# A decoder block on one core: GpSimd's element-wise work on VectorE, attention's loads a step sooner, the last block's end in two groups of positions

## The chip, the cores and the metric

The kernel runs on one core of one Trainium2 chip. The metric is the device time of one execution in microseconds; several runs are taken and their median is compared. The engines are called as the profile calls them: PE (TensorE), DVE (VectorE), ACT (ScalarE), POOL (GpSimd) and SP (SyncE, which issues the DMAs).

## The reference

One block of a hybrid decoder over 2048 positions of width 1024, in float32. A projection of the normalised input feeds gated linear attention (4 heads, in chunks) and a short gated convolution side by side; both go through one output projection and are added to the input; a SwiGLU feed-forward layer of width 2816 follows, and a last RMSNorm.

```python
h = rmsnorm(x, norm1_g[l])
proj = h @ w_in[l]
p_q, p_k, p_v, p_g, p_a, c_b, c_c, c_h = jnp.split(proj, splits, axis=-1)
...
gate_logits = (p_a @ w_gate_up[l] + b_gate[l]).astype(jnp.float32)
log_a = (jax.nn.log_sigmoid(gate_logits) / GATE_NORMALIZER).reshape(bsz, seq, GLA_HEADS, GLA_DK)
o = gla_chunked(q, k, v, log_a)
o = rmsnorm(o, gla_norm_g[l]).astype(x.dtype)
o = o * jax.nn.silu(p_g.reshape(bsz, seq, GLA_HEADS, GLA_DV))
...
o_conv = c_b * causal_depthwise_conv(u, conv_w[l])
```

After that come `x + concat(o_gla, o_conv) @ w_out`, the second norm, `silu(h @ w_gate) * (h @ w_up)` times `w_down` added to it, and the last norm.

## The kernel before

The 2048 positions are four blocks of 512; two blocks make a half. The stages run in the order opening, in_proj of half 0, in_proj of half 1 with the attention of half 0 beside it, the attention of half 1 beside out_proj(0), out_proj(1), then ffn_up and ffn_down of half 0 and of half 1, and `last_unit`, the last two columns of features of half 1 with the final norm.

All large products are float32 made of two parts in the faster format: every operand is split into a high part (ACT, line 193) and the rest (DVE, line 194), and each step is three matmuls (lines 460 to 462; 1220, 1221 and 1223 in out_proj) of 128x512. `unit` computes a 2 by 2 arrangement of blocks with seven products in place of eight, so sums and differences of operands are made ahead: `combine` (its `subtract`, line 359) for the normalised input, lines 1332 to 1336 in `ffn_up` for the feed-forward's hidden values, line 435 for the weights. Results leave the eight PSUM banks through ACT (line 500) or DVE (line 489).

The order of instructions on each engine is made once, when the program is built: a scheduler with an estimate of times merges the streams, and each engine then runs its list strictly in turn. SP issues every load (line 148) and store (line 151) in one such list. Side work, such as attention and norms, stands in generators in `background`; `tick()` takes one step of them between products. The step counts therefore decide where in PE's list a chunk stands.

Attention, `gla_half`, takes 8 chunks of 128 positions per half. A step makes the scores of a chunk, the next one finishes the chunk before (`gla_finish`: transposes `ot`, line 1178, gate, split, store to `sgla`), loads the next chunk (`gla_load`: 14 loads, two exponentials on ACT, lines 1105 and 1106, and two multiplications on DVE) and makes this chunk's outputs. `gate` and `forget_gate` (lines 1011 to 1024) make the decays that these loads read. out_proj(1) reads attention back from `sgla` as `op`.

The sums of squares for a norm: ACT squares a column (line 1201) and POOL adds it to `ssx` (line 1202); a matmul with ones (`rs` or `tot`) adds over features, and the factor is spread by transposes `rb_ps`. `last_unit` computes two columns for block 2 (j = 0), then for block 3 (j = 1), each of 18 matmuls of 128x512, sums squares, and scales all eight columns of each block before storing them (line 1480).

## Time and profile before

| | us |
|---|---|
| median of 3 runs | 2055.72 (2054.32 to 2055.76) |
| the profiled execution | 2050.15, span 2048.4, clock 0.996 |
| busy: PE, DVE, ACT, POOL | 2021.6, 1549.0, 971.7, 335.4 |
| opening and in_proj(0), to about | 250 |
| in_proj(1) with attention of half 0, to about | 475 |
| attention of half 1 beside out_proj(0), out_proj(1) from about | 667 |
| feed-forward, half 0 | 755 to 1380 |
| feed-forward, half 1 | 1380 to 2010 |
| `last_unit`'s last matmul of a column | 2033.2 |

The span is the time between the first and the last instruction of the profiled execution, so it is a little under that execution's own time. The rows of the profile name line, engine, operation and tiles; "idle before" with an arrow tells what ended the engine's wait.

### The profile page before, as it was taken

To read this page: it belongs to the slowest core of one execution; us is meant where nothing else is said; L and a number is where in the kernel's file an instruction comes from. 1 tells how busy PE (TensorE), PEld (TensorE's weight loads), DVE (VectorE), ACT (ScalarE), POOL (GpSimd) and SP (SyncE) were. 2 spreads that over 40 slices of the span, in tenths; PEclk is the share of its full clock that TensorE was granted. 3 is DMA by queue.
4 is the path that set the end of the run, shared out by engine and by line. 5 is a ranking of instruction groups with operands and counts; after the bars stand their busy time and mean duration, and the time that the engine had idled before them with its cause. 6 is when DMAs were issued, how large, how long until landed. Compare 5 with 4: busy or idle time off the path is not lost.

```text
span 2048.4 us, 26987 instructions
## 1 busy us (share of the span) xinstructions
PE 2021.6 (99%) x9271; PEld 1662.2 (81%) x9271; DVE 1549.0 (76%) x2533; ACT 971.7 (47%) x1930; POOL 335.4 (16%) x218
## 2 busy tenths in 40 slices
PE   9999999999999999999999999999999999999997
PEld 8788878887888888888788888877888888888886
DVE  7888967558744797778777688877777768778884
ACT  6664556755533344444444452334534443453344
POOL 0000000000002451222222112200311321211213
PEclk9999999999999999999999999999999999999998
DMA  7356886425586873546445576576444434586663
GB/s 262 123 201 215 295 301 188 132 85 160 180 307 233 324 270 134 194 150 216 176 145 193 212 285 250 188 277 273 155 169 170 167 136 170 185 328 221 236 231 114
DMA packets 189738, 422.54 MB, mean 206 GB/s; under 512 B 19904, under 2 KB 65184, under 8 KB 180128
## 3 DMA queue, kind: packets, MB, share of 16 engines
q1 hardware_dynamic: 189600, 420.81, 58.5%
q8 instruction: 73, 1.20, 0.2%
q14 instruction: 65, 0.53, 0.1%
HBM read 276.02 MB, written 144.70 MB: 205 GB/s over the span
## 4 chain that ended last, share of the span: by engine, by line
PE 87%; DVE 4%; DMA 4%; ACT 2%; issue 1%; SPq 1%; POOL 0%; DVEq 0%; ACTq 0%; POOLq 0%
PE mm L460 25%; PE mm L462 25%; PE mm L461 25%; PE mm L1220 2%; PE mm L1221 2%; PE mm L1223 2%; DMA raw<-in_wffn_dram 1%; DVE wq L194 1%; DVE h L894 1%; PE a_ps L976 1%; PE mm L756 1%; PE mm L758 1%; PE mm L757 1%; DMA raw<-in_win_dram 1%; PE o_ps L1144 1%
## 5 line engine op out<-in xcount | busy, mean ns | idle before, releaser
L460 PE MATMUL mm<-op,wq 128*128 128x512 f32 x2467 | 961.5, 392 | 10.9 <-ACT c L500 5.0
L461 PE MATMUL mm<-op,wq 128*128 128x512 f32 x2467 | 959.7, 390 | 0.2 <-DVE op L194 0.2
L462 PE MATMUL mm<-op,wq 128*128 128x512 f32 x2467 | 948.7, 390 | 0.9 <-DVE wq L194 0.6
L193 ACT ACTIVATE wq<-raw 128x512 fp32r<-128x512 f32 (+2 forms) x612 | 355.7, 587 | 582.5 <-PE mm L462 461.3
L194 DVE TENSOR_TENSOR wq<-raw,wq 128x512 fp32r<-128x512 f32 (+2 forms) x612 | 446.8, 736 | 165.1 <-ACT wq L193 163.5
L460 PEld LDWEIGHTS mm<-op,wq 128*128 128x128 f32 x2467 | 463.5, 188 | 115.3 <-ACT c L500 6.8
L462 PEld LDWEIGHTS mm<-op,wq 128*128 128x128 f32 x2467 | 463.5, 188 | 99.6 <-DVE wq L194 2.7
L461 PEld LDWEIGHTS mm<-op,wq 128*128 128x128 f32 x2467 | 463.6, 188 | 96.4 <-DVE op L194 1.7
L1202 POOL TENSOR_TENSOR ssx<-ssx,q 128x512 f32<-128x512 f32 x52 | 75.7, 1473 | 866.4 <-ACT q L1201 866.2
L489 DVE TENSOR_TENSOR c<-mm,c 128x512 f32<-128x512 f32 x196 | 134.6, 687 | 52.3 <-PE mm L462 44.9
L489 DVE TENSOR_TENSOR y<-mm,y 128x512 f32<-128x512 f32 x185 | 126.3, 686 | 47.8 <-PE mm L462 47.5
L435 DVE TENSOR_TENSOR raw<-raw 128x512 f32<-128x512 f32 (+2 forms) x192 | 151.9, 794 | 2.9
L1336 POOL TENSOR_TENSOR t<-c,c 128x512 f32<-128x512 f32 x44 | 74.4, 1690 | 434.8 <-DVE c L1332 406.9
L500 ACT ACTIVATE c<-mm 128x512 f32<-128x512 f32 x198 | 115.6, 587 | 17.5 <-PE mm L462 13.9
L435 DVE TENSOR_TENSOR s<-raw 128x512 f32<-128x512 f32 (+2 forms) x96 | 62.0, 645 | 52.0 <-DMA raw<-in_wffn_dram 36.5
L1220 PE MATMUL mm<-op,wq 128*128 128x512 f32 x256 | 101.2, 396 | 0.0
L1221 PE MATMUL mm<-op,wq 128*128 128x512 f32 x256 | 99.7, 390 | 0.0
L193 ACT ACTIVATE wq<-s 128x512 fp32r<-128x512 f32 (+2 forms) x96 | 56.3, 586 | 90.9 <-PE mm L462 88.2
L1418 POOL TENSOR_TENSOR y<-x,y 128x512 f32<-128x512 f32 x32 | 57.7, 1803 | 230.4 <-DVE y L489 181.3
L1223 PE MATMUL mm<-op,wq 128*128 128x512 f32 x256 | 80.0, 390 | 0.0
L435 DVE TENSOR_TENSOR raw<-s,raw 128x512 f32<-128x512 f32 (+2 forms) x96 | 69.8, 727 | 2.0
L552 ACT ACTIVATE c<-c 128x512 f32<-128x512 f32 x78 | 49.2, 631 | 34.7 <-DVE c L489 32.7
(229 smaller groups left out, 1788.5 us busy)
## 6 DMA issues: line engine op xcount, KB each, us to landing
raw<-in_wffn_dram SPq DMA_DIRECT2D x44, 1024.0 KB, 6.1
sa_B<-so SPq DMA_DIRECT2D x47, 512.0 KB, 4.3
op<-sa_B SPq DMA_DIRECT2D x47, 512.0 KB, 6.9
raw<-in_win_dram SPq DMA_DIRECT2D x22, 1024.0 KB, 5.5
sa_T<-so SPq DMA_DIRECT2D x44, 512.0 KB, 3.8
op<-sa_T SPq DMA_DIRECT2D x44, 512.0 KB, 6.4
raw<-in_wdown_dram SPq DMA_DIRECT2D x24, 768.0 KB, 5.8
sx<-y SPq DMA_DIRECT2D x48, 256.0 KB, 4.4
```

Source lines behind the costliest of these rows:

```text
L193: last_hi[:] = [act.activation(hi, src, AF.Copy)]
L194: last_lo[:] = [dve.tensor_tensor(lo, src, hi.bitcast(F32), ALU.subtract)]
L435: dve.tensor_tensor(*args)
L460: pe.matmul(o[:], wh, xh, start=first and k == 0, stop=False, skip_group_check=True)
L461: pe.matmul(o[:], wh, xl, start=False, stop=False, skip_group_check=True)
L462: return pe.matmul(o[:], wl, xh, start=False, stop=k == n - 1, skip_group_check=True)
L489: last_plus[:] = [dve.tensor_tensor(t[:], o[:], t[:], ALU.add)]
L500: last_out[:] = [act.activation(t[:], o[:], AF.Copy)]
L1202: pool.tensor_tensor(ssq[:], ssq[:], q[:], ALU.add)
L1220: pe.matmul(o[e, j][:], wh, m[:, 0, :], start=k == 0, stop=False)
L1221: pe.matmul(o[e, j][:], wh, m[:, 1, :], start=False, stop=False)
L1223: pe.matmul(o[e, j][:], wl, ops[k][j][:, 0, :], start=False, stop=k == KD - 1)
```

## The change

Six edits: (1) `subtract` in `combine`, (2) the sums of squares, (3) the four differences of `ffn_up` and (4) the last add of `ffn_down` go from POOL to DVE. (5) `gla_load` is cut in two: `gla_fetch` issues the loads, a step sooner, right behind the scores of the chunk before and ahead of `gla_finish`; `gla_scaled` has the exponentials and multiplications and stays where they were; one more `yield` stands at the start. (6) `last_unit` is written anew with an order of its own on each engine: block 2 (`j0`) as a whole, then the first 256 positions of block 3 (`p0`) and the last 256 (`p1`) one after the other. POOL keeps two sums and eight scales there, and stores are issued from SP and ACT.

```diff
 
         def subtract(y, a, b):
             with behind(last_plus if with_marks else []):
-                (dve if with_marks else pool).tensor_tensor(y, a, b, ALU.subtract)
+                dve.tensor_tensor(y, a, b, ALU.subtract)
 
         fetch()
         fetch()
@@ -1075,19 +1075,22 @@
         chunks = [(b, t) for b in (2 * half, 2 * half + 1) for t in range(PT)]
         with tc.issue_after(last_silu[0].ins):
             tables = act.preload_act_table_set("natural_log_exp_and_others")
+        fetched = gla_fetch(*chunks[0])
+        yield
         with tc.issue_after(tables.ins):
-            nxt = gla_load(*chunks[0])
+            cur = gla_scaled(*fetched)
         yield
         o = None
         for n, (b, t) in enumerate(chunks):
-            cur = nxt
             s = gla_scores(b, t, *cur)
             yield
+            if n + 1 < len(chunks):
+                fetched = gla_fetch(*chunks[n + 1])
             if o is not None:
                 yield from gla_finish(*chunks[n - 1], *o)
+            o = gla_outputs(b, t, *s)
             if n + 1 < len(chunks):
-                nxt = gla_load(*chunks[n + 1])
-            o = gla_outputs(b, t, *s)
+                cur = gla_scaled(*fetched)
             yield
         yield from gla_finish(b, t, *o)
         done.add((b, t))
@@ -1096,12 +1099,15 @@
     decays = {}
     done = set()
 
-    def gla_load(b, t):
+    def gla_fetch(b, t):
         s = slice(t * P, (t + 1) * P)
         kq, e, vt, g = [bt(n, (P, 4, P)) for n in ("kq", "ee", "vt", "gt")]
         for dst, src in ((kq, s_kq[b]), (e[:, 2:4, :], s_d[b]), (vt, s_v[b]), (g, s_g[b])):
             for i, r in enumerate(src):
                 load(dst[:, i, :], r[:, s])
+        return kq, e, vt, g
+
+    def gla_scaled(kq, e, vt, g):
         act.activation(e[:, 0:2, :], e[:, 2:4, :], AF.Exp, scale=-1.0 / 16.0)
         act.activation(e[:, 2:4, :], e[:, 2:4, :], AF.Exp, scale=1.0 / 16.0)
         dve.tensor_tensor(kq[:, 0:2, :], kq[:, 0:2, :], e[:, 0:2, :], ALU.mult)
@@ -1199,7 +1205,7 @@
         else:
             q = tt("q")
             act.activation(q[:], y, AF.Square)
-            pool.tensor_tensor(ssq[:], ssq[:], q[:], ALU.add)
+            dve.tensor_tensor(ssq[:], ssq[:], q[:], ALU.add)
 
     def build_mix(half):
         def pair(b, k):
@@ -1333,7 +1339,7 @@
             b11, b12, b21, b22 = [sg[r, j] for r in range(2) for j in range(2)]
             t1, t2, t3, t4 = [bt(n) for n in ("t1", "t2", "t3", "t4")]
             for y, p, q in ((t1, b12, b11), (t2, b22, t1), (t3, b22, b12), (t4, b21, t2)):
-                pool.tensor_tensor(y[:], p[:], q[:], ALU.subtract)
+                dve.tensor_tensor(y[:], p[:], q[:], ALU.subtract)
             values = [("B11", b11), ("B21", b21), ("B22", b22)]
             if half == 1 and m >= LAST_GROUP:
                 values.append(("B12", b12))
@@ -1415,7 +1421,7 @@
                     elif last:
                         store(s_x1[2 * half + j][d0 + r][:], yy)
                 for yy, x1 in xs:
-                    pool.tensor_tensor(yy, x1[:], yy, ALU.add)
+                    dve.tensor_tensor(yy, x1[:], yy, ALU.add)
         if half == 0:
             ahead[:] = [finish_later(half)]
 
@@ -1444,86 +1450,169 @@
...
+        HB = PB // 2
+        parts = {"j0": (0, 0, PB), "p0": (1, 0, HB), "p1": (1, HB, HB)}
+        order = {}
+        def then(eng, issue):
+            with behind([order[eng]] if eng in order else []):
+                order[eng] = issue()
+            return order[eng]
...
+        def spread(part, copied=True):
+            rb = rbs[part] = bank("rb_ps")
+            j, _, n = parts[part]
+            with behind([order[pe]]):
+                for t in range(n // P):
+                    order[pe] = pe.transpose(
+                        rb[:, t * P : (t + 1) * P], reps[part][:, t, :], ident[:]
+                    )
+            if copied:
+                copy_of(part)
+        def copy_of(part):
+            j, _, n = parts[part]
+            copies[part] = ssq[j][:, sl(part)]
+            then(act, lambda: act.activation(copies[part], rbs[part][:, 0:n], AF.Copy))
+        def scale(part, d, eng, queue):
+            j, _, n = parts[part]
+            by = rbs[part][:, 0:n] if eng is dve else copies[part]
+            yy = y[d, j][:, sl(part)]
+            then(eng, lambda: eng.tensor_tensor(yy, yy, by, ALU.mult))
+            with behind([order[act]] if queue is nc.scalar else []):
+                queue.dma_start(out[2 + j, :, d, sl(part)], yy)
+        def columns_of(part, r):
+            j, _, n = parts[part]
+            o = bank()
+            with behind([order[pe]] if pe in order else []):
+                for i in range(2):
+                    p = columns[j][i]
+                    for k in range(len(b12)):
+                        cs = slice(k * P, (k + 1) * P)
+                        wq = w[2 * r + i]
+                        for wi, xi in ((0, 0), (0, 1), (1, 0)):
+                            order[pe] = pe.matmul(
+                                o[:, 0:n], wq[:, wi, cs], p[k][:, xi, sl(part)],
+                                start=i == 0 and k == 0 and wi + xi == 0,
+                                stop=i == 1 and k == len(b12) - 1 and wi == 1,
+                                skip_group_check=True,
+                            )
+            return o
...
+        taken("j0", 0, columns_of("j0", 0))
+        summed("j0", 0, pool)
+        gained_in("j0", 0)
+        taken("j0", 1, columns_of("j0", 1))
+        summed("j0", 1, dve)
+        gained_in("j0", 1)
+        taken("p0", 0, columns_of("p0", 0))
+        summed("p0", 0, pool)
+        add_up("j0", ssq[0])
+        factors("j0")
+        gained_in("p0", 0)
+        taken("p0", 1, columns_of("p0", 1))
+        spread("j0")
+        summed("p0", 1, dve)
+        gained_in("p0", 1)
+        scale("j0", 0, dve, sp)
+        for d in (2, 4, 5, 6):
+            scale("j0", d, pool, sp)
+        taken("p1", 0, columns_of("p1", 0))
+        add_up("p0", ssq[1])
+        factors("p0", lambda: scale("j0", 1, dve, sp))
+        gained_in("p1", 0)
+        summed("p1", 0, dve)
+        o = columns_of("p1", 1)
+        spread("p0", copied=False)
+        add_up("p1", ssq[1], last=False)
+        taken("p1", 1, o)
+        add_up("p1", q[1, 1], first=False)
+        for d in (3, 7):
+            scale("j0", d, dve, sp)
+        factors("p1", *[partial(scale, "p0", d, dve, sp) for d in (0, 1)])
+        copy_of("p0")
+        gained_in("p1", 1)
+        for d in (2, 5, 6, 7):
+            scale("p0", d, pool, ac)
+        scale("p0", 3, dve, sp)
+        spread("p1", copied=False)
+        scale("p0", 4, dve, sp)
         for d in range(KD):
+            scale("p1", d, dve, ac if d % 2 else sp)
```

The functions left out keep their work: `add_up` sums over features, `factors` makes the reciprocal root and its copy `rep` for one part, `taken` adds a column and squares it, `summed` adds the squares up.

Line numbers move by 6 in the attention and out_proj code (1105 becomes 1111, 1179 becomes 1185, 1245 becomes 1251, 1202 becomes 1208). POOL's list falls from 205 rows to 16.

On ACT, in the list around the second gate: `L1105` and `L1106` (then `L1111` and `L1112`) are the exponentials of a chunk, `L500` the eviction of a PSUM bank, `L193` splits. Before:

```order
L193 ACTIVATE wq<-raw 128x512 [waits DVE_49]
L193 ACTIVATE wq<-raw 128x512 [waits PE_49]
L193 ACTIVATE wq<-raw 128x512 [waits DMAHW7_49,PE_49]
L1023 ACTIVATE el<-g_4745 128x4 [waits DVE_49]
L1105 ACTIVATE ee<-ee 128x256 [waits DMAHW5_49,DMAHW4_49]
L1106 ACTIVATE ee<-ee 128x256 [waits Activation_49]
L500 ACTIVATE c_4872<-mm 128x512 [waits DVE_49]
L1021 ACTIVATE em<-g_4842 128x4 [waits DVE_49]
```

and now:

```order
L500 ACTIVATE c_4854<-mm 128x512 [waits DVE_49,PE_49]
L1023 ACTIVATE el<-g_4724 128x4 [waits DVE_49]
L1014 ACTIVATE g_4824<-g_4824,ones 128x512 [waits Activation_49]
L193 ACTIVATE wq<-raw 128x512 [waits DVE_49]
L193 ACTIVATE wq<-raw 128x512
L1014 ACTIVATE g_4871<-g_4871,ones 128x512 [waits Activation_49]
L193 ACTIVATE wq<-raw 128x512 [waits DMAHW7_49,PE_49]
L1111 ACTIVATE ee<-ee 128x256 [waits DMAHW5_49,DMAHW4_49]
L193 ACTIVATE wq<-s_4971 128x512 [waits PE_49]
L1112 ACTIVATE ee<-ee 128x256 [waits Activation_49]
```

The eviction that stood right behind a pair of exponentials, and so behind their load, now stands ahead of the next pair; splits of weights stand behind and between them.

On DVE, where attention ends and out_proj(0) runs out: `osb<-ot` takes the last chunk's transposes, `osb<-osb,gt` makes the part that is stored, `y<-y,mm` are out_proj's evictions. Before:

```order
L1171 TENSOR_TENSOR osb<-o_ps,hsq 128x512
L1245 TENSOR_TENSOR y<-y,mm 128x512 x4
L1179 SCALAR_TENSOR_TENSOR osb<-ot,sml,gt 128x512
L194 TENSOR_TENSOR wq<-raw,wq 128x512
L194 TENSOR_TENSOR osb<-osb,gt 128x512
L194 TENSOR_TENSOR wq<-raw,wq 128x512 x3
L1245 TENSOR_TENSOR y<-y,mm 128x512 x4
L194 TENSOR_TENSOR wq<-raw,wq 128x512 x3
L256 TENSOR_SCALAR rb_6780<-tot 128x512
```

and now:

```order
L1185 SCALAR_TENSOR_TENSOR osb<-ot,sml,gt 128x512
L194 TENSOR_TENSOR osb<-osb,gt 128x512
L194 TENSOR_TENSOR wq<-raw,wq 128x512
L1251 TENSOR_TENSOR y<-y,mm 128x512 x3
L1208 TENSOR_TENSOR ssx_5989<-ssx_5989,q 128x512
L1251 TENSOR_TENSOR y<-y,mm 128x512
L1208 TENSOR_TENSOR ssx_5990<-ssx_5990,q 128x512
L194 TENSOR_TENSOR wq<-raw,wq 128x512
L1208 TENSOR_TENSOR ssx_5989<-ssx_5989,q 128x512
L1208 TENSOR_TENSOR ssx_5990<-ssx_5990,q 128x512
L194 TENSOR_TENSOR wq<-raw,wq 128x512
L256 TENSOR_SCALAR rb_6780<-tot 128x512
```

Before, two columns of out_proj's evictions (x4 each) stand around or behind the last chunk's rows and further ones follow; now one column follows and the sums of squares, which POOL had, stand between. On PE the last chunk's four transposes stand 96 large matmuls ahead of out_proj(1)'s first one before, and 37 now.

On PE, the end of the program: `rs` sums squares over features, `rb_ps` are the transposes that spread the factors, the other rows are a column's matmuls. Before:

```order
L461 MATMUL mm<-op,wq 128x512
L462 MATMUL mm<-op,wq 128x512
L460 MATMUL mm<-op,wq 128x512
L461 MATMUL mm<-op,wq 128x512
L462 MATMUL mm<-op,wq 128x512
L1454 MATMUL rs<-ones,q 128x1 [waits Activation_49]
L1454 MATMUL rs<-ones,q 128x1 x3
L1474 MATMUL rb_ps<-ident,rep 128x128 [waits DVE_49]
L1474 MATMUL rb_ps<-ident,rep 128x128 x3
```

and now:

```order
L1541 MATMUL mm<-op,wq 128x256 x18
L1481 MATMUL rs<-ones,ssx_17441 128x1 [waits DVE_49]
L1481 MATMUL rs<-ones,ssx_17441 128x1
L1541 MATMUL mm<-op,wq 128x256 x18
L1511 MATMUL rb_ps<-ident,rep 128x128 [waits DVE_49]
L1511 MATMUL rb_ps<-ident,rep 128x128
L1481 MATMUL rs<-ones,ssx_17441 128x1 [waits DVE_49]
L1481 MATMUL rs<-ones,ssx_17441 128x1
L1481 MATMUL rs<-ones,q 128x1 [waits Activation_49]
L1481 MATMUL rs<-ones,q 128x1
L1511 MATMUL rb_ps<-ident,rep 128x128 [waits DVE_49,PE_49]
L1511 MATMUL rb_ps<-ident,rep 128x128
```

The last column is 18 matmuls of 256 positions, and what follows the last matmul is two rows for each thing where there were four; the other 256 positions' transposes stand there too.

119 lines of the change are left out of this document (53 added, 66 removed).

## The prediction

> **What bounds the kernel now.** I read the page's first part, then the chain of waits, the waits by engine, the busy time by stage, and the timelines of the three places that the change reorders.
>
> ```profile
> PE 2021.6 (99%) x9271; PEld 1662.2 (81%) x9271; DVE 1549.0 (76%) x2533; ACT 971.7 (47%) x1930; POOL 335.4 (16%) x218
> PE 87%; DVE 4%; DMA 4%; ACT 2%; issue 1%; SPq 1%; POOL 0%; DVEq 0%; ACTq 0%; POOLq 0%
> ```
>
> TensorE is busy 99% of the span and makes 87% of the chain that ended last; POOL has no share in the chain. So work that leaves POOL gains nothing by itself. Time can only come from PE's idle time, from what lies behind PE's last matmul, or from the number and speed of matmuls.
>
> ```profile
> PE mm L460 <- ACT c L500: 5.0, 3, 3.0
> PE mm L460 <- ACT wq L193: 1.2, 3, 0.5
> PE rs L226 <- POOL ssx L1202: 0.3, 1, 0.3
> ...
> 645.00:667.00 22.00, 22.00 (x100) 18.21 (x98) 8.06 (x11) 4.84 (x10) 5.77 (x4) 1.00 1.01 360
> 667.00:755.00 88.00, 88.00 (x386) 72.17 (x385) 71.32 (x78) 35.21 (x60) 47.29 (x30) 1.00 0.90 317
> 755.00:1380.00 625.00, 623.11 (x2750) 513.25 (x2749) 493.49 (x751) 267.61 (x489) 131.37 (x80) 1.00 0.56 200
> ```
>
> The waits (total us, times, longest) are few; the largest is one stall of 3.0 us behind an eviction on ACT (L500). Of all POOL work PE waited 0.3 us. In the stage rows the columns after the window's length are PE, weight loads, DVE, ACT and POOL busy, then the clock, the DMA share and GB/s; 88.00/386 gives 0.228 us per matmul of 128x512.
>
> **1. The gate, at 473 us.**
>
> ```profile
> 472.31 0.79 SPq L148 DMA_DIRECT2D ee<-sd  x2
> 474.79 0.42 ACT L1105 ACTIVATE ee<-ee 128x256 f32<-128x256 f32 x1 [1.02 <-DMA ee<-sd]
> 475.56 0.58 ACT L500 ACTIVATE c<-mm 128x512 f32<-128x512 f32 x1
> 476.19 0.53 PE L460 MATMUL mm<-op,wq 128*128 128x512 f32 x1 [3.01 <-ACT c L500]
> 476.20:479.60 3.40, 3.40 (x9) 2.68 (x10) 3.40 (x8) 0.21 (x1) 0.00 (x0) 0.55 0.43 104
> ```
>
> ACT stands at the exponentials of a chunk whose load was issued only at 472.31; behind them in its queue is the eviction for which PE waits. That costs PE 3.01 us. Then the clock falls: in the next 3.40 us, at a granted clock of 0.55, 9 matmuls run where 3.40/0.228 = 15 would, so 6 x 0.228 = 1.4 us more. Together 4.4 us. The change fetches the chunk a step sooner, and in its ACT order that eviction stands ahead of the exponentials. A chunk's 14 loads at 0.79/2 = 0.4 us are 5.5 us of SP's queue; they now stand ahead of the previous chunk's two stores, which wait that much and which nobody reads before out_proj. Against the gain: weight splits (L193 wq) now stand behind the exponentials, on which PE also waits, and the whole attention moves a step later, so all its meetings are dealt anew. As the price of those I take 1.0, near the 1.2 us that all waits on such splits cost before. Term: -3.4 (bounds -4.4, and 0 if another wait fully takes its place).
>
> The Trainium skill, "TensorE: Matmul & The Clock Gate", section "What's actually happening", says that the array falls to half clock after an idle window of about 3.4 us. The trace agrees about so (a wait of 3.01 us sufficed); by that rule waits of under 3 us cost only themselves.
>
> **2. The end of attention, at 645 us.** The extra step of the attention generator pushes its last chunk behind: before, the last transposes `ot` stand 96 matmuls ahead of out_proj(1)'s first; in the change's PE order 37. So the slack falls from 96 x 0.228 = 21.9 to 37 x 0.228 = 8.4 us, plus three matmuls on the other block before the first that reads the new data: 9.1.
>
> ```profile
> 644.64 0.60 PE L1178 MATMUL ot<-ident,osb 128*128 128x128 f32 x4
> 645.87 0.74 DVE L1179 SCALAR_TENSOR_TENSOR osb<-ot,sml,gt 128x512 f32<-128x512 f32 x1
> 646.67 0.62 ACT L193 ACTIVATE gt<-osb 128x512 fp32r<-128x512 f32 x1
> 647.84 1.77 DVE L194 TENSOR_TENSOR osb<-osb,gt 128x512 fp32r<-128x512 f32 x1
> 649.64 0.51 SPq L151 DMA_DIRECT2D sgla<-osb  x1
> 653.08 3.66 SPq L148 DMA_DIRECT2D op<-sgla  x7
> DMA to landing us min/median/max: 3.4/6.0/6.9
> DMA to landing us min/median/max: 6.0/10.5/11.3
> ```
>
> What must pass in it: eviction, split on ACT and DVE, store, load. Before, from the end of `ot` at about 645.1 to the earliest landing of a load at 653.08 + 6.0 = 659.1 it took 14.0 us, hidden within 21.9. (The last two rows are landing times of the `sgla` transfers in 649 to 654 and of the `op` loads from 653 on.) At its best: 0.3 to start, 0.74 + 0.62 + 0.69 (the split without POOL beside it, as other 512-wide DVE rows below), 0.3 between them, 3.4 for the store and 3.4 for the load: 9.4. So PE waits 0.3 to 4.9 us, and at the long end the half clock adds 1.4: 0.3 to 6.3. I take +2.0, nearer the low end, since POOL no longer stretches the split (1.77 to 0.69) and DVE's rows just ahead of it are short. Later loads follow at the rate at which PE uses them, so the wait comes once.
>
> **3. POOL's work on DVE.** 52 sums of squares, 88 subtracts of ffn_up, 32 adds of ffn_down and 32 subtracts of `combine`: 204 operations.
>
> ```profile
> L1202 POOL TENSOR_TENSOR ssx<-ssx,q 128x512 f32<-128x512 f32 x52 | 75.7, 1473 | 866.4 <-ACT q L1201 866.2
> L1336 POOL TENSOR_TENSOR t<-c,c 128x512 f32<-128x512 f32 x44 | 74.4, 1690 | 434.8 <-DVE c L1332 406.9 <-DMA sa_B<-so 27.9
> L1418 POOL TENSOR_TENSOR y<-x,y 128x512 f32<-128x512 f32 x32 | 57.7, 1803 | 230.4 <-DVE y L489 181.3 <-DMA x<-sx 48.5 <-ACT wq L193 0.6
> ...
> L489 DVE TENSOR_TENSOR y<-mm,y 128x512 f32<-128x512 f32 x185 | 126.3, 686 | 47.8 <-PE mm L462 47.5
> L194 DVE TENSOR_TENSOR wq<-raw,wq 128x512 fp32r<-128x512 f32 x422 | 336.0, 801 | 155.0 <-ACT wq L193 153.8
> L435 DVE TENSOR_TENSOR raw<-raw 128x512 f32<-128x512 f32 x130 | 116.3, 897 | 1.9
> L194 DVE TENSOR_TENSOR op<-t,op 128x512 fp32r<-128x512 f32 x8 | 9.4, 1172 | 2.4 <-ACT op L193 2.2
> ```
>
> On DVE such an operation takes 0.686 us (the row of L489) where POOL takes 1.5 to 1.8: 204 x 0.686 = 139.9 us more on DVE. But DVE operations with two SBUF inputs are longer than 686 ns on the mean, and only while POOL runs beside them: 422 x 0.115 + 130 x 0.211 + 8 x 0.486 = 48.5 + 27.4 + 3.9 = 79.8 us in these three rows alone, which should vanish with POOL's work. DVE then goes from 1549 to at most 1549 + 139.9 - 79.8 = 1609 us, 79% of the span. The tightest stage is 667 to 755: 71.3 + 30 x 0.686 = 91.9 us, more than its 88, if nothing got shorter; less the 3.9 (all eight are there) and POOL's share of the rest there, 47.3/335.4 x 75.9 = 10.7, it is 77.3. It fits. In 755 to 1380: 493.5 + 80 x 0.686 = 548 of 625 without any relief. So I cost this part at 0: PE's matmuls cover it. What it costs if the cover is gone is the second rival. Gone is only the wait on POOL's `ssx`: -0.3. Bounds: -4 (the small waits of the FFN also vanish) to +4 (the 91.9 - 88 of the tight stage).
>
> **4. The end.**
>
> ```profile
> 2032.74 12.21 SPq L151 DMA_DIRECT2D out_dram<-y  x15
> ...
> 2033.40 0.25 PE mm L462
> 2033.75 0.69 DVE L1508 TENSOR_TENSOR y<-mm,y 128x512 f32<-128x512 f32 x1 [0.49 <-PE mm L462]
> 2034.47 0.63 ACT L1511 ACTIVATE q<-y 128x512 f32<-128x512 f32 x1 [3.13 <-DVE y L1508]
> 2035.16 1.05 PE L1454 MATMUL rs<-ones,q 128*128 128x1 f32 x8 [1.52 <-ACT q L1511]
> 2037.46 0.43 DVE L1467 COPY rep<-py 128x512 f32<-128x512 f32 x1
> 2037.94 1.12 PE L1474 MATMUL rb_ps<-ident,rep 128*128 128x128 f32 x4 [1.73 <-DVE rep L1467]
> 2039.79 3.68 DVE L1480 TENSOR_TENSOR y<-y,rb_ps 128x512 f32<-128x512 f32 x6 [1.90 <-ACT ssx L1475]
> out_dram<-y SPq DMA_DIRECT2D x16, 256.0 KB, 2.5
> L460 PEld LDWEIGHTS mm<-op,wq 128*128 128x128 f32 x2467 | 463.5, 188 | 115.3 <-ACT c L500 6.8
> ```
>
> Now the last column ends at 2033.65 and the run 2048.4: 14.75 us of add, square, sum, factors, transposes, 8 scales and 16 stores. In the change only 256 positions go through that at the end. Halving what depends on the width: add 0.1 + 0.35; square 0.05 + 0.42 (an exponential of 256 in part 1's fence took that); four sums 0.53 + 0.05; factors from the end of `rs`, 2036.22, to the transposes, 2037.94: 1.72, less half the copy's 0.43 is 1.50; two transposes 0.56; eight scales between half of 3.68/6 and 0.42: 8 x 0.36 = 2.9; last store's issue 0.45, landing 2.5; and 1.0 to the run's end, as before (2032.74 + 12.21 + 2.5 = 2047.45, against 2048.4). With 0.5 between steps: 10.9 us, so -3.85. The other half's and the first block's stores, 3 MB, must be out before: at the 360 GB/s of 645 to 667 that is 8.7 us, and by the order they start two narrow columns, some 4.3 us, ahead of the last column's end and are out at +4.4, when the last scales start. POOL's four scales of 256 run beside DVE's and may stretch them, bound +1.
>
> PE's stream itself: fewer `rs` ahead of the last column (6 rows in the order instead of 12, each two matmuls in the trace at 1.05/8 = 0.13): 6 x 2 x 0.13 = 1.6 at half clock; at the full clock they are shorter, I take -1.3. 36 matmuls of 512 become 72 of 256, each weight loaded twice. At half the time each nothing changes; if the weight load of 0.188 us sets the pace it is 72 x 0.188 - 36 x 0.228 = +5.3. Against that: the eight `rs` matmuls, each with a 128x128 weight load of its own, come 0.13 apart at half clock, so 0.188 is a load's length and not its pace. I take 0.12 each, +0.5. Term: -1.3 + 0.5 - 3.85 = -4.6 (bounds -6 to +1.7).
>
> The Trainium skill, "TensorE: Matmul & The Clock Gate", sections "LDWEIGHTS (loading the stationary operand)" and "Back-to-back issue gap", gives 107 ns for a load of 128 columns and 262 cycles, 109 ns, for 256 columns of matmul. By it the 72 would take an estimated 7.9 us, no more than the 36; no run here shows a 256-wide one.
>
> **Sum.** -3.4 + 2.0 - 0.3 + 0 - 4.6 = -6.3 us. The profiled execution took 2050.15 us around its span of 2048.4 and lies 5.6 under the median of the runs. Taken off the profiled one it gives 2043.9; off the median of 2055.7, which is what is measured, 2049.4.
>
> **The rivals.**
>
> *Attention's end takes back what its start gives.* The wait in part 2 at its long end, 6.3, and a split that takes the place of the gate's stall (0 for -3.4): +6.3 - 0.3 - 4.6 = +1.4, 2057. For it: 9.1 us of slack against 14.0 as measured. Against: the stretched split and 1 us of DVE queue in those 14.0.
>
> *DVE's queue blocks: slower.* POOL could sit idle for its inputs at no cost; DVE takes its work in order. Of POOL's idle time 27.9 us ended with a store of `so` and 48.5 with a load of `x` (rows of part 3). Where such a wait now stands in DVE's queue, weight splits and evictions stand behind it. The 48.5 us are 1.5 per add, and a column of 24 matmuls lasts 5.5, so a late eviction is hidden as long as other banks are free; it decides from the point where a wait exceeds about one column. If a fifth of the 76.4 us comes through, +15: 2055.7 - 6.3 + 15 = 2064. Against: PE's waits on DVE are all under 2 us now, and the stages have 12% to spare.
>
> *Narrow matmuls paced by weight loads*: +4.8 on the sum, 2054.2.
>
> *The FFN's small waits go too*, as DVE's operations are shorter: -4 more, 2045.4. For it: PE loses a few us in waits on `c` and `wq` there; against: they are redealt, not removed.
>
> **How the numbers follow.** Forecast 0.50, attention's end 0.18, DVE's queue 0.14, weight loads 0.08, FFN 0.10. What this measurement tells from no change is 0.2%, 4.1 us. Faster by more: most of the forecast and all of the FFN case, 0.43 + 0.10, and little of the others: 0.55. Same: 0.07 of the forecast, 0.10 of attention's end, 0.07 of the weight loads: 0.24. Slower: 0.21. The forecast's own range is 2046 to 2053 (the gate's 0 to -4.4 and the end's bounds). For 8 in 10 it is widened to the FFN case below and past attention's end above, with part of DVE's queue: 2043.5 to 2060.
>
> **What would show it.** Gate: no PE idle over 1 us behind L500 near 473 and no window under full clock there. Attention's end: a PE wait on a load of `op<-sgla` at out_proj(1) of about 2 us. DVE: L194's mean for 128x512 near 690 ns, DVE's busy time under 1610, POOL with some ten operations. End: last column to end near 11 us, and 18 matmuls of 256 in 2.0 to 2.2 us. I am wrong if PE's waits on DVE rows, or on weights split late, grow by 6 us or more, or if the 256-wide matmuls take over 0.15 us each.

## The result, and the profile after

| | before | after |
|---|---|---|
| median, us | 2054.38 (2050.22 to 2055.76, 6 runs) | 2043.03 (2041.94 to 2045.20, 6 runs) |
| ratio | | 0.9951, 95% interval 0.9941 to 0.9961 |
| profiled execution, us | 2050.15, span 2048.4 | 2043.05, span 2041.3 |

The change is faster by 10.1 us by the ratio (8.0 to 12.1); 6.3 were forecast. The ratio is not the quotient of the two medians, which lie 11.4 us apart; differences below go by the ratio unless medians are named. The median lies 0.5 us under the low end of the forecast's range, and the kernel before ran 1.3 us under the 2055.7 from which the forecast was taken off. The page of the changed kernel, its busy times and its chain:

```profile
PE 2016.8 (99%) x9295; PEld 1661.9 (81%) x9295; DVE 1534.8 (75%) x2752; ACT 976.4 (48%) x1936; POOL 11.0 (1%) x17
PE 92%; DMA 3%; DVE 3%; ACT 1%; issue 0%; SPq 0%; DVEq 0%; ACTq 0%
```

POOL has gone from 335.4 us to 11.0, and DVE, with 219 operations more (POOL's 204 and some of the new end), is busy for 14 us less. The waits of PE (total, times, longest) and two stages of the same profile (window, its length, then PE, weight loads, DVE, ACT, POOL, clock, DMA share, GB/s):

```profile
PE mm L460 <- ACT c L500: 4.2, 5, 1.7
PE rb_ps L1511 <- DVE rep L1503: 2.7, 2, 2.4
PE mm L460 <- ACT op L193: 2.1, 1, 2.1
PE mm L462 <- DVE wq L194: 1.2, 1, 1.2
...
PE rs L1481 <- DVE ssx L1566: 1.0, 1, 1.0
...
PE mm L1226 <- DMA op<-sgla: 0.4, 1, 0.4
```

```profile
667.00:755.00 88.00, 88.00 (x385) 72.01 (x385) 68.01 (x110) 33.71 (x56) 0.00 (x0) 1.00 0.97 353
755.00:1380.00 625.00, 624.19 (x2762) 515.74 (x2761) 486.45 (x835) 271.05 (x493) 0.00 (x0) 1.00 0.56 203
```

The stall of 3.0 us behind L500 is gone, and the longest such wait is 1.7; the forecast wait on `op<-sgla` is there with 0.4 us. Two lines belong to the end, both waits on DVE: the one on `rep` was there before with 1.7 and has grown to 2.7, the one on `ssx` is new. The row of `op` from L193, at 271 us, has the same 2.1 in the kernel before.

Where the 7.1 us between the two profiled spans went, from the times at which PE reaches the same places (read from the timelines; each place is the first matmul of its kind there):

| stretch | before, us | after, us | difference |
|---|---|---|---|
| start to the gate matmul of half 0 | 89.41 | 89.97 | +0.56 |
| to the last matmul of out_proj(1) | 666.06 | 664.89 | -1.17 |
| to the first spread of the second norm | 29.81 | 28.35 | -1.46 |
| to the second spread | 31.76 | 31.76 | 0 |
| the rest of half 0's feed-forward and the start of half 1's, to the final norm's first spread | 690.94 | 688.59 | -2.35 |
| to the last column's last matmul | 525.26 | 524.19 | -1.07 |
| last matmul's start to the end of the span | 15.19 | 13.58 | -1.61 |

So the gain is spread over four places (the last two rows are both the end), and 3 us more of the ratio lie in runs that these two profiles don't show. The experiments take these apart.

### The profile page after: what moved, and what is told of

The parts are those of the page before. It is cut to its first block, busy times and chain, and to the rows that moved or that the text cites. A ratio compares the mean times of both kernels' runs of the same rounds, so it can differ in the third digit from the quotient of the medians.

```text
span 2041.3 us, 26875 instructions
## 1 busy us (share of the span) xinstructions
PE 2016.8 (99%) x9295; PEld 1661.9 (81%) x9295; DVE 1534.8 (75%) x2752; ACT 976.4 (48%) x1936; POOL 11.0 (1%) x17
## 4 chain that ended last, share of the span: by engine, by line
PE 92%; DMA 3%; DVE 3%; ACT 1%; issue 0%; SPq 0%; DVEq 0%; ACTq 0%
PE mm L460 25%; PE mm L462 25%; PE mm L461 25%; PE mm L1226 3%; PE mm L1227 3%; PE mm L1229 3%; PE mm L756 1%; PE a_ps L976 1%; PE mm L757 1%; PE mm L758 1%; PE o_ps L1148 1%; PE o_ps L1150 1%; PE mm L1541 1%; DVE wq L194 0%; PE sc L1124 0%
## 5 line engine op out<-in xcount | busy, mean ns | idle before, releaser
L193 ACT ACTIVATE wq<-raw 128x512 fp32r<-128x512 f32 (+2 forms) x612 | 357.4, 588 | 602.1 <-PE mm L462 486.7
L460 PEld LDWEIGHTS mm<-op,wq 128*128 128x128 f32 x2443 | 458.5, 188 | 109.6 <-ACT c L500 6.4
L462 PEld LDWEIGHTS mm<-op,wq 128*128 128x128 f32 x2443 | 458.5, 188 | 98.6 <-DVE wq L194 2.7
L461 PEld LDWEIGHTS mm<-op,wq 128*128 128x128 f32 x2443 | 458.7, 188 | 95.2 <-DVE op L194 1.5
L194 DVE TENSOR_TENSOR wq<-raw,wq 128x512 fp32r<-128x512 f32 (+2 forms) x612 | 386.0, 636 | 179.6 <-ACT wq L193 178.2
L500 ACT ACTIVATE c<-mm 128x512 f32<-128x512 f32 x198 | 115.3, 589 | 20.7 <-PE mm L462 16.7
L435 DVE TENSOR_TENSOR raw<-raw 128x512 f32<-128x512 f32 (+2 forms) x192 | 120.3, 632 | 2.2
L193 ACT ACTIVATE wq<-s 128x512 fp32r<-128x512 f32 (+2 forms) x96 | 56.4, 587 | 103.7 <-PE mm L462 98.0
L435 DVE TENSOR_TENSOR s<-raw 128x512 f32<-128x512 f32 (+2 forms) x96 | 60.8, 633 | 35.6 <-DMA raw<-in_wffn_dram 20.0
L194 DVE TENSOR_TENSOR op<-op 128x512 fp32r<-128x512 f32 x94 | 62.0, 684 | 3.6 <-ACT op L193 3.5
L194 DVE TENSOR_TENSOR wq<-s,wq 128x512 fp32r<-128x512 f32 (+2 forms) x96 | 60.8, 633 | 3.3 <-ACT wq L193 2.5
L435 DVE TENSOR_TENSOR raw<-s,raw 128x512 f32<-128x512 f32 (+2 forms) x96 | 60.8, 634 | 1.4
L193 ACT ACTIVATE op<-op 128x512 fp32r<-128x512 f32 x94 | 54.6, 620 | 7.2 <-DMA op<-sa_T 3.7
L1226 PEld LDWEIGHTS mm<-op,wq 128*128 128x128 f32 x256 | 48.1, 188 | 11.3 <-issue 1.6
```

The lines of the kernel that those rows point to most:

```text
L193: last_hi[:] = [act.activation(hi, src, AF.Copy)]
L194: last_lo[:] = [dve.tensor_tensor(lo, src, hi.bitcast(F32), ALU.subtract)]
L435: dve.tensor_tensor(*args)
L460: pe.matmul(o[:], wh, xh, start=first and k == 0, stop=False, skip_group_check=True)
L461: pe.matmul(o[:], wh, xl, start=False, stop=False, skip_group_check=True)
L462: return pe.matmul(o[:], wl, xh, start=False, stop=k == n - 1, skip_group_check=True)
```

## The experiments

The edits are numbered as in the change: (1) `combine`, (2) sums of squares, (3) and (4) the feed-forward's differences and adds, (5) attention's loads, (6) the end. Every kernel was timed beside the kernel before on the same chip.

| run | what | median, us | ratio to before |
|---|---|---|---|
| e1 | before, again | 2053.24 | 0.9999 (0.9991 to 1.0008) |
| e2 | (1) to (4) | 2048.41 | 0.9981 (0.9969 to 0.9993) |
| e3 | (5) | 2055.89 | 1.0014 (1.0005 to 1.0023) |
| e4 | (6) | 2051.55 | 0.9988 (0.9979 to 0.9997) |
| e5 | (1) to (4), (6) | 2046.38 | 0.9965 (0.9953 to 0.9977) |
| e6 | (1) to (5) | 2045.88 | 0.9964 (0.9952 to 0.9976) |
| e7 | (1), (2), (5) | 2046.45 | 0.9965 (0.9953 to 0.9977) |
| e8 | (1), (5) | 2047.91 | 0.9975 (0.9965 to 0.9984) |
| the change | (1) to (6) | 2043.03 | 0.9951 (0.9941 to 0.9961) |
| e9 | change, one add of the end on PE | 2042.67 | 0.9945 (0.9932 to 0.9958) |
| e10 | e9, copies of the end on ACT | 2044.18 | 0.9949 (0.9936 to 0.9962) |
| e11 | change, end without POOL | 2044.56 | 0.9954 (0.9940 to 0.9969) |
| e12 | (1), (2), (5), (6) | 2046.27 | 0.9966 (0.9954 to 0.9978) |

### The kernel before, again, and what its runs differ by

No edit.

> The kernel before, unchanged, for its spread (2050.2 to 2055.8 so far) and a second profile. Theory A: the runs at 2054 to 2056 carry one or two stalls that the profiled one of 2050.15 did not have, and this profile shows where (a PE wait of some us, or a second piece of half clock). Theory B: they are slower evenly, by clock or by opening, with no single place. Ratio to before 1.000.

The second profile has a span of 2051.5 us, 3.1 more than the first. Two short windows of it, with the same columns as above:

```profile
274.12:277.53 3.41, 3.22 (x8) 2.54 (x9) 3.41 (x7) 3.05 (x6) 0.00 (x0) 0.50 1.04 377
478.92:482.33 3.41, 3.19 (x8) 2.51 (x9) 3.41 (x9) 0.38 (x2) 0.00 (x0) 0.50 0.42 119
```

The second piece of half clock is the one of the prediction, behind the stall at the gate. The first isn't in the earlier profile: it follows a wait of 2.45 us for `op` at 271, where half 1's projection begins. In the earlier profile that wait is 2.10 us (the row of `op` from L193 shown above, which the prediction's rows leave out). It stands in every profile taken here (1.7 to 2.7 us); with the half clock after it in all but the first one of before and the one of the change. The piece costs about 3.41 x 0.5 = 1.7 us; the rest of the 3.1 is 0.8 in the first 90 us and 0.8 in a longer wait at 310. Theory A holds in the main, as far as one more profile shows it: the first profile of before is one of its better executions, so beside it the change gains 7.1 us and beside the runs 10.1.

### POOL's work on DVE alone

Edits (1) to (4), such as

```diff
-                pool.tensor_tensor(y[:], p[:], q[:], ALU.subtract)
+                dve.tensor_tensor(y[:], p[:], q[:], ALU.subtract)
```

> Only POOL's 204 operations on DVE, attention's loads and the end as before. If the sum of the prediction holds (0, bounds -4 to +4): 2050 to 2055 in the median, DVE busy under 1610 us, L194 of 128x512 near 690 ns. Theory B, that this part carries the gain since operations that POOL no longer stretches release stalls of the feed-forward: 2045 to 2049. Rival of DVE's blocked queue: over 2058.

This is theory B's range. By the ratio it is -3.9 us (-6.4 to -1.4). DVE's splits and sums in this profile, and the tightest stage:

```profile
L194 DVE TENSOR_TENSOR wq<-raw,wq 128x512 fp32r<-128x512 f32 x422 | 289.7, 688 | 159.3 <-ACT wq L193 157.4
...
667.00:755.00 88.00, 88.00 (x386) 72.14 (x386) 70.00 (x113) 36.54 (x61) 0.00 (x0) 1.00 0.94 343
```

801 ns have become 688, and the tight stage holds 35 operations more at 1.3 us less of busy time (71.32 before). No blocked queue shows. On PE's path the stretch to the second norm's spread is 28.37 us (29.79 in the second profile of before), and the feed-forward of half 0 688.69 (691.04): 3.8 us together, which is the whole gain by the ratio.

### Attention's loads alone

Edit (5).

```diff
+            if n + 1 < len(chunks):
+                fetched = gla_fetch(*chunks[n + 1])
             if o is not None:
                 yield from gla_finish(*chunks[n - 1], *o)
```

> Only attention's loads a step sooner, POOL and the end as before. By the prediction -3.4 + 2.0 and by the trace after about -2.6: 2051 to 2053, with no stall at the gate, and with POOL stretching the last split (1.8 us) a wait on op<-sgla of 1 to 3 us. If the loads alone carry nothing (another stall takes the place): 2054 to 2056.

The median lies in the second range, and as it says another stall takes the place; but the loads don't carry nothing, they cost 2.9 us (1.0 to 4.7). The gate's stall is gone as foreseen, and a worse one stands at 762. The wait on `op<-sgla` is 0.40 us where 1 to 3 were expected. The timeline of this run:

```profile
750.07 1.74 POOL L359 TENSOR_TENSOR t<-h,t 128x512 f32<-128x512 f32 x1
751.83 0.33 SPq L151 DMA_DIRECT2D sfT<-t  x1
...
755.74 2.62 SPq L148 DMA_DIRECT2D h<-sfB  x4
758.00 3.91 ACT L193 ACTIVATE op<-h 128x512 fp32r<-128x512 f32 x6 [2.96 <-DMA h<-sfB]
763.05 0.61 ACT L193 ACTIVATE wq<-raw 128x512 fp32r<-128x512 f32 x1
763.71 0.50 PE L460 MATMUL mm<-op,wq 128*128 128x512 f32 x1 [2.03 <-ACT wq L193]
766.39 1.75 DVE L194 TENSOR_TENSOR wq<-raw,wq 128x512 fp32r<-128x512 f32 x1
768.20 0.80 PE L462 MATMUL mm<-op,wq 128*128 128x512 f32 x1 [3.75 <-DVE wq L194]
```

Read it from the bottom. PE waits for a weight split; the split stands on ACT behind six splits of `op<-h`; these wait for loads, and the loads stand in SP's queue behind the store of POOL's last difference, made at 750 to 752. The waits of 2.03 and 3.75 us and 6.8 us of half clock behind them make the stretch to the second norm's spread 36.3 us where it was 29.8.

### The end alone

Edit (6).

```diff
+        parts = {"j0": (0, 0, PB), "p0": (1, 0, HB), "p1": (1, HB, HB)}
...
+                                o[:, 0:n], wq[:, wi, cs], p[k][:, xi, sl(part)],
```

> Only the end in two groups of positions, the rest as before. By the trace after it is worth 14.75 - 13.3 us behind the last column and 1.2 us on PE ahead of it, 2.7 us: 2051 to 2052. If the end is worth what was predicted (4.6): 2049 to 2050.

By the ratio -2.5 us (-4.3 to -0.6); last matmul to end 13.64 us, as in the change. It is the smaller of the two sizes.

### The change without the loads, and without the end

The whole change without edit (5), with one yield and one call as before:

```diff
-        fetched = gla_fetch(*chunks[0])
-        yield
         with tc.issue_after(tables.ins):
-            cur = gla_scaled(*fetched)
+            nxt = gla_load(*chunks[0])
```

> The change without its edit on attention's loads (POOL's work on DVE and the new end). Theory A, the parts add up: -5.4 of DVE alone and -2.3 of the end alone from 2053.8 give 2046.1, with the gate's stall of about 3 us still there. Theory B, the loads carry nothing even with DVE: as the whole change, 2043.

2046.38: the parts add up, 0.9981 x 0.9988 = 0.9969 beside 0.9965. So beside DVE's edits and the new end the loads are worth 0.9951/0.9965, 2.9 us, and alone they cost as much. The two intervals overlap by 0.0008; e6 below beside e2, which also differ in the loads alone, gives 3.5 us the same way.

The whole change without edit (6), `last_unit` as before:

```diff
-            scale("p1", d, dve, ac if d % 2 else sp)
+            scale(1, d, None if d in (2, 5) else rb1)
```

> The change without its new end. Theory A: the whole change's 2043.0 plus 2.3 to 2.7 for the end, 2045.3 to 2045.7, last column to end 14.7 us. If the end is worth more once DVE is free of POOL (4.6 as predicted): 2047.6.

2045.88: 2.9 us above the change, 2.7 by the ratios, with intervals that overlap. The end alone gave 2.5, and e5 beside e2 gives 3.3. So the end is worth about the same with DVE free of POOL as without, 2.5 to 3.3, and 4.6 appears in none of the three.

### What makes the loads slow alone

Edits (5), (1) and (2): the feed-forward stays on POOL.

```diff
-                (dve if with_marks else pool).tensor_tensor(y, a, b, ALU.subtract)
+                dve.tensor_tensor(y, a, b, ALU.subtract)
...
-            pool.tensor_tensor(ssq[:], ssq[:], q[:], ALU.add)
+            dve.tensor_tensor(ssq[:], ssq[:], q[:], ALU.add)
```

> Attention's loads a step sooner, and of POOL's work only what belongs to norms (the differences of combine and the sums of squares) on DVE; the feed-forward's differences and adds stay on POOL, the end as before. Theory A, that the loads alone were slow since splits of weights stood on ACT behind six splits that waited for loads of what POOL had made late (waits of 2.0 and 3.8 us at 761 to 768 and half clock after them): no such wait, 2046 to 2049. Theory B, that the later attention itself makes these waits: they stay, 2053 to 2056.

No wait of PE is left at 750 to 770, and the median is 2046.45.

Edits (5) and (1) alone: the first two lines of that diff.

> Attention's loads a step sooner and of POOL's work only the differences of combine on DVE. If it is these differences, on POOL, that came late: no wait over 1 us at 761 to 768, 2047 to 2050. If it is the sums of squares beside them that stretch DVE's splits there (1.75 in place of 0.69 us): a wait of 2 to 4 us stays, 2051 to 2055.

2047.91. The same place in this run, DVE making the last difference:

```profile
747.25 0.68 DVE L359 TENSOR_TENSOR t<-h,t 128x512 f32<-128x512 f32 x1
747.96 0.32 SPq L151 DMA_DIRECT2D sfT<-t  x1
...
748.85 3.93 SPq L148 DMA_DIRECT2D h<-sfB  x4
751.78 2.64 ACT L193 ACTIVATE op<-h 128x512 fp32r<-128x512 f32 x4 [1.09 <-DMA h<-sfB]
...
762.32 0.50 PE L462 MATMUL mm<-op,wq 128*128 128x512 f32 x1 [1.01 <-DVE wq L194]
```

The last difference is stored 3.9 us sooner, at 747.96 where it was 751.83, and ACT gets past its six splits some 5 us sooner; PE's 5.8 us of waits shrink to 1.0. So it is the differences of `combine`, 32 operations, that turn the loads from a loss into a gain. That they do it by coming sooner is read from these rows: the order of ACT's list changes with the edit as well. With the sums of squares on DVE as well (e7) the last 1.0 goes there too; the two medians lie 1.5 us apart, within the intervals.

### The end, taken apart

The timeline of the end of the changed kernel:

```profile
2024.34 5.07 POOL L1526 TENSOR_TENSOR y<-y,ssx 128x512 f32<-128x512 f32 x4 [3.16 <-ACT ssx L1520]
2025.65 2.38 PE L1541 MATMUL mm<-op,wq 128*128 128x256 f32 x18
2027.35 0.94 DVE L1503 COPY rep<-py 128x256 f32<-128x256 f32 x1
2028.21 1.48 DVE L1566 TENSOR_TENSOR ssx<-ssx,q 128x256 f32<-128x256 f32 x1
2029.61 0.41 DVE L1555 TENSOR_TENSOR y<-mm,y 128x256 f32<-128x256 f32 x1
2029.74 0.61 PE L1481 MATMUL rs<-ones,ssx 128*128 128x1 f32 x4 [0.96 <-DVE ssx L1566]
2032.48 2.83 POOL L1526 TENSOR_TENSOR y<-y,ssx 128x256 f32<-128x256 f32 x4 [3.07 <-ACT ssx L1520]
2032.49 0.86 DVE L1503 COPY rep<-py 128x256 f32<-128x256 f32 x1
2033.50 0.66 PE L1511 MATMUL rb_ps<-ident,rep 128*128 128x128 f32 x2 [2.37 <-DVE rep L1503]
```

The last column ends at 2028.0. Its eviction (L1555) could start then and starts at 2029.61, behind a copy and an add that run while POOL does its four scales. In e9 PE adds up these squares instead:

```diff
-        summed("p1", 0, dve)
...
         add_up("p1", ssq[1], last=False)
+        add_up("p1", q[1, 0], first=False, last=False)
```

> The whole change, and in the end p1's first squares are added up by two more matmul rows in place of DVE's add, which took 1.48 us beside POOL and held the last eviction back. Theory A, that this stretched add set the end: last column to end of span 13.3 - 1.2 = 12.1 us, median 2041.8. Theory B, that stores set it: end and median as the change, 2043.0.

From the last matmul's start to the end of the span it is 12.31 us (13.58 in the change): the 1.27 us of theory A, in the profile. In the median 0.4 is left, which the runs can't tell from nothing.

In e10 ACT also makes the copies of p0 and p1:

```diff
+                then(
+                    act,
+                    lambda: act.activation(rep[:, 0:n, :], c.to_broadcast([P, n, P]), AF.Copy),
+                )
```

> As the run before, and the copies rep of p0 and p1 are made by ACT (which has no part in DVE's and POOL's contention) in place of DVE, 0.94 and 0.86 us there. Theory A: the copies take 0.3 to 0.45 us, the end is 12.1 - 0.4 = 11.7 us, median 2041.2 to 2041.5. Theory B: as the change.

The copies take 0.41 and 0.42 us, and the last scales of DVE end 0.6 us sooner after the last matmul; but the span ends 12.28 us after it, as in e9. From the last scale to the end it is 4.9 us now and 4.4 in e9: ACT's queue is still issuing its eight stores 2.3 us after the last scale, 1.5 in e9 and in the change. So here the stores set the end, theory B. The median, 2044.18 over 2040.05 to 2046.53, tells nothing.

In e11 POOL has no scale at all:

```diff
-            scale("j0", d, pool, sp)
+            scale("j0", d, dve, sp)
...
-            scale("p0", d, pool, ac)
+            scale("p0", d, dve, ac)
```

> The whole change with all scales of the end on DVE, POOL idle beside it. Theory A, that POOL stretches DVE there: rep of 128x256 takes 0.45 us or less (0.94 and 0.86 now), the add of 128x256 0.43 (1.48 now); DVE has 4 x 0.69 + 4 x 0.37 = 4.2 us more, so the end is 13.3 - 2 + 4.2 = 15.5 at most, median 2043 to 2046. Rival, that the copy is slow by itself (it reads one value again and again): rep stays at 0.86 or more.

The timeline of this run:

```profile
2030.25 0.29 DVE L1503 COPY rep<-py 128x256 f32<-128x256 f32 x1
2030.46 0.42 DVE L1566 TENSOR_TENSOR ssx<-ssx,q 128x256 f32<-128x256 f32 x1
2030.79 0.42 DVE L1555 TENSOR_TENSOR y<-mm,y 128x256 f32<-128x256 f32 x1
```

Copy and add take 0.29 and 0.42 where they took 0.94 and 1.48, so it was POOL beside them and not the operation; the eviction, which reads PSUM, took 0.41 and takes 0.42. But DVE's own eight scales then stand in front, and the end is 13.9 us beside 13.6 in the change. In the profiles POOL is worth its place in the end by these 0.3 us, which the runs can't tell from nothing, only not beside these two operations.

### The feed-forward left on POOL

The whole change but for edits (3) and (4):

```diff
-                dve.tensor_tensor(y[:], p[:], q[:], ALU.subtract)
+                pool.tensor_tensor(y[:], p[:], q[:], ALU.subtract)
...
-                    dve.tensor_tensor(yy, x1[:], yy, ALU.add)
+                    pool.tensor_tensor(yy, x1[:], yy, ALU.add)
```

> The whole change, but the 120 differences and adds of the feed-forward stay on POOL. If stretched DVE work in the feed-forward costs nothing, since PE's matmuls cover it (the prediction's 0 for it): 2043 to 2044, as the whole change, with L194 of 128x512 above 720 ns on the mean and the stretch from the norms' end at 785 us to the same point of the second half within 0.5 us of the change's 688.6 but for stray waits. If it costs: 2045.5 or more.

2046.27: by the ratios it costs 3.1 us (0.9966 against 0.9951; the intervals overlap by 0.0007). But the same two edits are all that lies between e7 and e6, and there they bring 0.2 us (0.9965 against 0.9964). What they are worth is therefore not clear of noise. L194's mean is 752 ns. In the profile, of an execution of 2048.10 us and so 1.8 above the median, the stretch between the spreads that the expectation names is 692.4 us, 3.8 longer than in the change, and all but some 0.6 of that is one place, where the second feed-forward begins. The timeline there:

```profile
1379.02 0.69 DVE L435 TENSOR_TENSOR s<-raw 128x512 f32<-128x512 f32 x1 [5.52 <-DMA raw<-in_wffn_dram]
...
1380.36 0.68 DVE L489 TENSOR_TENSOR y<-mm,y 128x512 f32<-128x512 f32 x1
...
1381.10 0.50 PE L460 MATMUL mm<-op,wq 128*128 128x512 f32 x1 [2.21 <-DVE y L489]
```

and in the changed kernel:

```profile
1376.26 0.69 DVE L435 TENSOR_TENSOR s<-raw 128x512 f32<-128x512 f32 x1 [3.98 <-DMA raw<-in_wffn_dram]
...
1377.60 0.68 DVE L489 TENSOR_TENSOR y<-mm,y 128x512 f32<-128x512 f32 x1
...
1378.34 0.50 PE L460 MATMUL mm<-op,wq 128*128 128x512 f32 x1 [0.68 <-DVE y L489]
```

DVE stands at a combination of weights whose load has not landed, with the eviction that PE needs behind it. By DVE's wait the load is 1.5 us later than in the change, PE's wait grows from 0.68 to 2.21, and half clock (1.7 us) follows it in this run and not in the other. Why it comes later there was not followed up; the same wait of 2.0 to 2.2 us stands in e4 and e7, and one of 0.6 to 0.9 in before, e1, e3 and e8, which have this work on POOL too. Over all profiles the stretch is 688.4 to 689.2 us with the work on DVE (seven profiles) and 689.0 to 693.4 with it on POOL (seven). So with edits (3) and (4) the long cases are absent; it isn't shown that stretched operations cost PE anything elsewhere.

## Why the prediction was right, and where not

Forecast were -1.4 us for the loads, -0.3 for POOL's work and -4.6 for the end; the runs give about -2.9, -3.9 and -2.5 to -3.3. Two terms are too small and one is too large, so the sum of 6.3 is nearer to 10.1 than it would be if all had erred one way: that much of it is luck.

**The gate: right on the stall, short on what takes its place.** The timeline in the changed kernel:

```profile
474.21 0.58 ACT L500 ACTIVATE c<-mm 128x512 f32<-128x512 f32 x1
...
474.84 0.50 PE L460 MATMUL mm<-op,wq 128*128 128x512 f32 x1 [0.45 <-ACT c L500]
```

The eviction at 474.21 stands ahead of the exponentials' load (issued at 474.94), as the order said; PE waits 0.45 us there in place of 3.01. But the waits were redealt: 0.97 at 302, 1.17 at 298 and 0.77 at 490 are new in the change, 0.7 at 384 and 0.2 at 309 went. Up to out_proj(1)'s end the change gained only 1.2 us on the first profile of before, which has one piece of half clock there, and 3.2 on e1 (668.07), which has two. That waits of under 3 us cost only themselves, as the prediction took from the rule of the clock, does not hold: in e1 the wait of 2.45 us at 271 is followed by 3.41 us at half clock. Forecast for the loads were -3.4 + 2.0 = -1.4; beside DVE's edits the runs give -2.9.

**Attention's end: the place was right, the size too big.** PE waits for `op<-sgla` at 666.8, 0.35 us. The chain in the changed kernel, timeline:

```profile
656.72 0.60 PE L1184 MATMUL ot<-ident,osb 128*128 128x128 f32 x4
657.36 0.75 DVE L1185 SCALAR_TENSOR_TENSOR osb<-ot,sml,gt 128x512 f32<-128x512 f32 x1 [1.58 <-PE ot L1184]
658.81 0.69 DVE L194 TENSOR_TENSOR osb<-osb,gt 128x512 fp32r<-128x512 f32 x1 [0.70 <-ACT gt L193]
659.53 0.51 SPq L151 DMA_DIRECT2D sgla<-osb  x1
...
666.79 0.47 PE L1226 MATMUL mm<-op,wq 128*128 128x512 f32 x1 [0.35 <-DMA op<-sgla]
```

From the end of `ot` at 657.3 to PE's start it is 9.5 us: the low end of the bounds, 9.4. The value of 2.0 was taken above that end without a row that asked for it. Of the 14.0 measured before, DVE's late starts and the stretched split made some 2.2 us; the other 2.3 came from the transfers, since the last store landed 3.4 us after its issue and the first load 6.0, and here 2.7 and 4.4. It was not POOL's move that shortened this: in e3, with all of POOL's work still there, the chain is as short.

```profile
659.43 0.69 DVE L194 TENSOR_TENSOR osb<-osb,gt 128x512 fp32r<-128x512 f32 x1 [0.70 <-ACT gt L193]
...
667.46 0.47 PE L1226 MATMUL mm<-op,wq 128*128 128x512 f32 x1 [0.40 <-DMA op<-sgla]
```

**POOL's work on DVE: the cost was right, the value wrong.** DVE did not become a bound, and the operations that POOL stretched gave back 1549.0 + 139.9 - 1534.8 = 154 us, more than the 79.8 that three rows showed. But "PE's matmuls cover it, 0" was the step that failed: e2 gives -3.9 us by the runs and -3.8 by the profiles, at the forecast's bound of -4. Of it 1.4 us lie between out_proj(1)'s end and the second norm's first spread, which takes 28.35 to 28.37 us in all nine profiles with the differences of `combine` and the sums of squares on DVE and 29.8 to 30.0 in before, e1 and e4. Half of the reason was in the trace of before. Its small waits at 761, 764, 1010, 1014 and 1382 were listed as a rival of 0.10, and no longer stand, or stand shorter. That rival was the better forecast: its 2045.4 is nearest to the time. The other half could not be read there: the differences of `combine` on POOL, stored 4 us later than on DVE, are what would have made the loads a loss (e3 against e8).

**The end: mis-sized.** -4.6 forecast; between the profiles of e2 and e5, which differ in this edit, -2.1 (0.55 ahead of the last matmul, 330.31 to 329.76 from the final norm's second spread, and 1.56 behind it, 15.12 to 13.56), and 2.5 to 3.3 by the runs. The narrow matmuls were right: the last column's 18 start at 2025.65 to 2027.75, 0.12 us apart as was taken, not 0.188 (their 2.38 us hold the full length of the last one). The estimate from the Trainium skill, "TensorE: Matmul & The Clock Gate", section "Back-to-back issue gap", 0.109, is a little low. The sum of 10.9 us behind the last column became 13.3: the eviction starts 1.6 us after the last matmul, where 0.1 was put, and from the sums to the transposes it is 2.4, where 1.5 was. It priced copy, add and eviction as if DVE were alone, in a stretch in which POOL still had eight scales; e9 shows 1.27 us of it. The same contention that part 3 priced for POOL's old work was left out where the change keeps POOL.

**The rivals.** Attention's end (2057) and the weight loads (2054) did not come. DVE's blocked queue came nowhere with DVE's new work; its mechanism stands at one place, at 1378, with an old operation (L435) in front, and shows its price there: 0.7 to 2.2 us, and the half clock.

**What stays open:** how often the half clock falls behind the wait at 271 in runs without a profile, and with it how the 10.1 us divide; what edits (3) and (4) are worth, 3.1 us in one pair of runs and 0.2 in the other; and which of the feed-forward's small waits went by shorter operations and which by another order (half 0 took 689.4 and 689.0 us in e3 and e8 as well, where all of its work was still on POOL).

## What to carry to other kernels

An engine that is off the critical path can still decide where work stands on the path: the chain to follow is from its last result through the store, the load and whatever in-order queue waits for that load. An edit that is a loss alone can be a gain beside another (the loads, +2.9 and about -2.9 us), so a part that looks bad alone should be tried beside the others. When VectorE work is priced beside GpSimd, price operations with two SBUF inputs, and a plain copy, as stretched for as long as GpSimd runs, also in the last few microseconds: here the splits of L194 took 801 ns on the mean in place of 688, an add of 256 columns 1.48 us in place of 0.42 and a copy 0.94 in place of 0.29.

## What the hardware showed that was not expected

The granted clock halves by windows of 3.413 us on a fixed grid, and a good half of a window without work is enough. The Trainium skill, "TensorE: Matmul & The Clock Gate", section "What's actually happening", has free-running windows of 3413 ns and asks for an idle one; the windows agree with these traces, the condition does not. In the traces every piece of half clock starts a whole number of 3.413 us after the clock's first record. Leaving out the last piece of each program, which starts within 15 us of its end and follows windows with as little as 1.4 us of idle, each follows a window in which PE was idle for 56% or more, but for one in e9. Three pairs of windows on that grid, of the change, of e5 and of e2:

```profile
270.25:273.66 3.41, 1.56 (x7) 0.94 (x6) 1.29 (x2) 1.99 (x4) 0.00 (x0) 1.00 1.03 393
273.66:277.07 3.41, 2.89 (x11) 2.17 (x12) 3.14 (x6) 3.41 (x8) 0.00 (x0) 1.00 1.04 389
```

```profile
475.09:478.50 3.41, 1.49 (x7) 0.91 (x5) 3.41 (x7) 1.31 (x3) 0.00 (x0) 1.00 0.43 119
478.50:481.91 3.41, 1.91 (x8) 1.61 (x9) 3.41 (x10) 1.52 (x4) 0.00 (x0) 1.00 0.67 191
```

```profile
272.10:275.51 3.41, 1.50 (x5) 1.03 (x6) 2.77 (x5) 3.05 (x7) 0.00 (x0) 1.00 1.06 428
275.51:278.92 3.41, 3.41 (x9) 2.66 (x9) 3.41 (x7) 2.50 (x5) 0.00 (x0) 0.50 0.83 281
```

With PE busy for 1.56 or 1.49 us of the first window (third number) the second has clock 1.00; with 1.50 it has 0.50. In e5 the wait was 3.42 us long but lay across two windows and cost nothing more; in e10 one of 1.73 us with smaller gaps in the same window, 1.95 us together, halved the clock. Of some 40 windows with over 1.1 us of idle in 14 profiles, taken before the end, those with 1.81 us or less left the clock at 1.00, but for one (e9, 1.63 us), and those with 1.92 or more halved it, but for the one of e5 shown. PE's ends are modelled, so the limit is about 1.9 us and no sharper. A kernel that waits 2 us at one place so loses 1.7 us more in some executions and not in others, by where the grid falls, and two profiles of the same program differ by that much.
